# Second norm applied behind the up projection, GpSimd's sums moved to DMA and VectorE, residual and gate loads moved

## The chip, the core and the metric

The kernel runs on one core of a Trainium2 chip. The metric is the time of one execution in microseconds (us). A core has five engines with a queue each, worked off in order: PE (TensorE, matrix products), DVE (VectorE), ACT (ScalarE), POOL (GpSimd) and SP (SyncE, which here only issues DMAs). DMAs issued by SP are those of the profile's queue q1 (hardware_dynamic), those issued by POOL are those of q0 (software_dynamic); in this kernel every DMA of POOL adds its source to its destination.

## What is computed

One layer over 1056 tokens (1024 of a prompt, 8x4 new ones), model width 1024, all in float32:

```
xn = rmsnorm(x, norm1_g);  proj = xn @ w_in          # q, k, v, xr, gr, ga_logit, gr_logit
att = window_attend(q, k, v, ...);  h = rglru(causal_conv(xr, ...))
rnn = (h * gelu(gr)) @ w_o_rnn
mix = (sigmoid(ga_logit) * (att @ w_o_attn) + sigmoid(gr_logit) * rnn) @ w_out
x = x + mix
hmid = relu(rmsnorm(x, norm2_g) @ w_up)              # 1024 -> 4096
x = x + (hmid * hmid) @ w_down                       # 4096 -> 1024
gate = sigmoid(rmsnorm(x, ple_norm_g) @ w_ple_gate)
x = x + gate * (p @ w_ple)
```

rmsnorm(x, g) = x * rsqrt(mean(x*x) + eps) * g, with the mean over the 1024 features of a token.

## The kernel before

Activations lie turned: features on the 128 partitions, the 1056 tokens along a row, so a 1024x1056 matrix is eight tiles [128, 1056]. Each float32 product is made of three matmuls, from a high part (a rounded copy, made by ACT) and a low part (the difference, made by DVE) of both factors: high*high, high*low, low*high.

**First half.** The projections go by chunks of 352 tokens: a chunk is 24 matmuls, and `linear` runs three chunks for one tile of weights. A helper, `Flow`, runs side work between chunks: a generator's `yield n` puts its rest n chunks later. `recur(j)`, j = 0 to 7, is nine chunks: the tiles of xr, gr and ga_logit, with the side work `gates`, whose matmuls (lines 844, 845) take all four PSUM banks `o` and are emptied by ACT (line 847). `turn_x` is side work from j = 2 on: for each of the eight feature tiles it loads x (`xi`), turns it on PE (lines 902, 906) through the same `o` banks, copies it by ACT (903) and stores it in DRAM (`x_dram`), to be read as the residual `X` later.

**Second half.** Ten stages of 28 steps follow: rnn (@ w_o_rnn), out (@ w_out), then up and down four times (here up0, down0, up1, ...; 1024 of the 4096 columns each). A stage is a 1024x1024 product by Strassen's scheme with seven products q = 0 to 6 of half-size blocks, each in four steps p = 0 to 3 of 24 matmuls with 264 tokens (lines 1422 to 1424). Step s of the whole is stage s // 28. `acc`, PSUM, has room for four steps' results.

- Weights: blocks A11, A12, A21, A22 are loaded by SP a stage ahead; their sums (S1 to S4) are made in `down_sums` (stages rnn, out, down: by ACT and POOL's adding DMAs, from eight steps ahead) or in `w_sums` (up0 on POOL, up1 to up3 on DVE). `w_high` (ACT, 1119) and `w_low` (DVE, 1124) split them four and three steps ahead.
- Activations: `b_sums` makes T1 to T4 in place from four blocks b11, b12, b21, b22 (`rnn`, `hid` or `xn` rows), on DVE (1137 to 1142); `b_split` (ACT 1156, DVE 1157) splits them into `ring`, for product q in the first two steps of product q - 1. In up0 the split rows also go to DRAM (`xc_dram`), from where up1 to up3 load them.
- `evacuate` takes a step's result one step later. In rnn it adds into `hid`, and `mix` multiplies by the opened gates (`sigma_of`) and adds `A` (POOL's DMA, 1326). Each gate half row is loaded by SP two steps before its use (1314) into one of four places (two `t`, two halves of `ssq`) and opened by ACT (1317). In out it adds into `X`; a part shared by three blocks is added by POOL's DMA (1247); `squares` has ACT square the finished half row and POOL add it into `ssq` (1180).
- `second_norm(th_)` (for one half of the tokens) sums `ssq` over partitions on PE (1338) and forms the root by ACT and DVE (1339, 245 to 252). `scaled_rows` (DVE, 1350) then makes xn = X * gain * root, from which up0's products start. In the up stages ACT applies Relu and Square to a finished row (1221, 1222).
- `differences` (POOL, 1267) prepares `X` for the down stages. `hooks` says at which step such work is called.

What stands in an engine's queue waits for what stands ahead of it there, so a late operand on DVE or ACT delays the evacuations behind it.

Of the kernel before, what the change touches and what calls it, by code (L numbers as in the profile page):

```python
# [18 lines left out]
P = 128  # L19
# [71 lines left out]
def trunk(ctx: ExitStack, tc: tile.TileContext, I, O):  # L91
# [150 lines left out]

    def rsqrt(r, ms, u):

        ACT.activation(r, ms, AF.Ln)
        ACT.activation(r, r, AF.Exp, scale=-0.5)
        newton(r, ms, u)

    def newton(r, ms, u):
        DVE.tensor_tensor(u, r, ms, op=ALU.mult)  # L250
        DVE.tensor_tensor(u, u, r, op=ALU.mult)  # L251
        DVE.scalar_tensor_tensor(r, u, 3.0, r, op0=ALU.subtract, op1=ALU.mult)

# [637 lines left out]
    def turn_x():  # L891
        for j in range(KT):
# [4 lines left out]
            yield 2  # L897
# [12 lines left out]
    for j in range(KT):  # L910
        if j == 2:
            flow.run(turn_x(), 1)
        recur(j)
# [137 lines left out]
    def kept_place(j2, th_):  # L1051
        return f"d{(2, 3, 0, 1)[j2] if th_ == 0 else (5, 7, 4, 6)[j2]}"
# [6 lines left out]
    def b_view(ph_, k2, kh_, th_):  # L1059

        kind, f = phases[ph_]
        if kind == "rnn":
            return [rnn[4 * kh_ + 2 * k2 + i][:, HALF[th_]] for i in range(2)]
        return [(xn if kind == "up" else hid)[k2 + 2 * kh_][th_]]

    units = {}

    def down_sums(s):

        ph_, at = divmod(s + 8, 28)  # L1070
        if not 0 <= ph_ < NPH or phases[ph_][0] == "up":
            return
# [27 lines left out]
    def w_sums(u):  # L1100
        ph_, q, p2 = u // 28, u % 28 // 4, u % 4 // 2
        if phases[ph_][0] != "up":
            return
        eng = POOL if phases[ph_][1] == 0 else DVE
        v = lambda n: w_view(ph_, n, p2)
        if q == 1:
            eng.tensor_tensor(v("A21"), v("A11"), v("A21"), op=ALU.subtract)
        elif q == 2:
            eng.tensor_tensor(v("S2"), v("A22"), v("S3"), op=ALU.subtract)
        elif q == 5:  # L1110
            eng.tensor_tensor(v("A11"), v("S2"), v("A11"), op=ALU.add)
# [17 lines left out]
    def b_sums(g, k2):  # L1129

        ph_, q = of_product(g)
        kind, f = phases[ph_]
        if kind == "up" and f:
            return
        for b11, b12, b21, b22 in zip(*(b_view(ph_, k2, kh_, th_) for kh_, th_ in ((0, 0), (0, 1), (1, 0), (1, 1)))):
            if q == 2:
                DVE.tensor_tensor(b12, b22, b12, op=ALU.subtract)
                DVE.tensor_tensor(b11, b12, b11, op=ALU.add)
            elif q == 4:
                DVE.tensor_tensor(b21, b21, b11, op=ALU.subtract)  # L1140
            elif q == 5:
                DVE.tensor_tensor(b11, b22, b11, op=ALU.subtract)  # L1142
# [56 lines left out]
    def evacuate(u, ps):  # L1199
# [9 lines left out]
        put = lambda to, of, op: DVE.tensor_tensor(to, of, ps, op=op)  # L1209
        if kind == "up":  # L1210
            if q == 0:
                ACT.copy(q11, ps)
                return
            if q == 1:
                ACT.copy(q12, ps)
            for to, of in (None, [(q11, q11)], [(q12, q12)], [(q22, q12)], [(q21, q22)], [(q22, q22), (q12, q12)], [(q12, q12)])[q]:
                put(to, of, ALU.add)
            h = {1: q11, 4: q21, 5: q22, 6: q12}.get(q)
            if h is not None:
                def squared_relu():  # L1220
                    ACT.activation(h, h, AF.Relu)
                    ACT.activation(h, h, AF.Square)
                flow.later(1, squared_relu)
            return
        if kind == "rnn":

            if q == 0:
                ACT.activation(q11, ps, AF.Identity, scale=-1.0)
                return
            if q == 1:  # L1230
                ACT.activation(q12, ps, AF.Identity, scale=-1.0)
            for to, of, op in (None, [(q11, q11, 0)], [(q12, q12, 1)], [(q22, q12, 0)], [(q21, q22, 1)],
                               [(q22, q22, 1), (q12, q12, 1)], [(q12, q12, 0)])[q]:
                put(to, of, (ALU.subtract, ALU.add)[op])
            if q in (1, 4, 5, 6):
                mix(p + 4 * (q in (4, 5)), q > 4)
            return
        if kind == "out":
# [71 lines left out]

    def loads_gate(j, th_):
        sig = sigmas[len(sigma_of) % 4]
        sigma_of[j, th_] = sig
        SP.dma_start(sig, s_dram[j, :, HALF[th_]])

    def opens_gate(j, th_):
        ACT.activation(sigma_of[j, th_], sigma_of[j, th_], AF.Sigmoid)
# [259 lines left out]
```

## Time and profile before

| | us |
|---|---|
| three runs | 1645.15, 1645.45, 1649.81; median 1645.45 |
| the profiled execution's own time | 1645.47 |
| its span in the profile (first to last instruction) | 1643.7 |
| PE busy in the span | 1560.7 (95%) |
| DVE / ACT / POOL busy | 1066.5 / 859.5 / 365.3 |
| mean granted TensorE clock | 0.984 of full speed |

The profiled execution stands within 0.1 us of the median, so what is read in it is taken off the median directly. PE is busy nearly all the time; what can be gained is where it is not. A granted clock of 1.00 is 2.4 GHz, 0.50 is 1.2 GHz. A stage's borders are found by counting PE's matmuls of lines 1422 to 1424, 672 to a stage.

### The profile page before, as it was taken

How to read it: one execution, taken by the hardware profiler on the slowest of the kernel's cores; microseconds unless marked ns; L12 is line 12 of the kernel's file. 1: busy time of each engine (PE TensorE's matmuls, PEld its weight loads, DVE VectorE, ACT ScalarE, POOL GpSimd, SP SyncE). 2: the span in 40 equal slices, each digit the busy share in tenths (PEclk: the TensorE clock that was granted, in tenths of full speed). 3: DMA queues.
4: the chain of work that ended last, by engine and by line, in shares of the span. 5: the costliest groups of instructions: out<-in, count | busy, mean ns of one | idle time of the engine just before them, and what ended most of it. 6: DMA issues, size and time to landing. Idle time of an engine off the chain costs nothing.

```text
span 1643.7 us, 28183 instructions
## 1 busy us (share of the span) xinstructions
PE 1560.7 (95%) x11488; PEld 1539.8 (94%) x11488; DVE 1066.5 (65%) x1428; ACT 859.5 (52%) x1360; POOL 365.3 (22%) x333
## 2 busy tenths in 40 slices
PE   6989999999899999997967999999999999999997
PEld 5889999999899999997967999999999999999997
DVE  6797565443234441887898888468846884689863
ACT  6555656776677765553444553445344534455441
POOL 4562225222123310220656120001000100012110
PEclk9999999999999999999997999999999999999999
DMA  5422112133232165798922793587358735880332
GB/s 176 78 81 68 53 68 79 52 97 109 89 106 77 42 205 209 151 262 205 199 107 86 287 182 112 203 288 127 113 203 290 125 114 201 292 174 2 99 91 75
DMA packets 177498, 229.30 MB, mean 140 GB/s; under 512 B 21556, under 2 KB 128228, under 8 KB 177352
## 3 DMA queue, kind: packets, MB, share of 16 engines
q1 hardware_dynamic: 148568, 195.83, 35.9%
q0 software_dynamic: 28800, 31.66, 12.0%
q8 instruction: 91, 1.49, 0.4%
q14 instruction: 39, 0.32, 0.1%
HBM read 158.22 MB, written 38.60 MB: 120 GB/s over the span
## 4 chain that ended last, share of the span: by engine, by line
PE 45%; DVE 4%; DMA 2%; issue 1%; ACT 0%; POOL 0%; DVEq 0%; POOLq 0%; ACTq 0%
PE acc L1423 13%; PE acc L1424 13%; PE acc L1422 13%; PE acc L1517 2%; PE acc L1519 2%; PE acc L1518 2%; DMA X<-shared 1%; DVE xn L1350 1%; DVE wul L1124 1%; DVE ring L1157 1%; PE acc L1477 0%; DVE X L1209 0%; DMA out_y_prompt<-yo 0%; POOL ssq L1180 0%; DVE hid L251 0%
## 5 line engine op out<-in xcount | busy, mean ns | idle before, releaser
L1422 PE MATMUL acc<-ring,wuh 128*128 128x264 f32 x2240 | 640.3, 286 | 19.0 <-DVE hid L1209 9.5
L1423 PE MATMUL acc<-ring,wuh 128*128 128x264 f32 x2240 | 642.2, 287 | 5.7 <-DVE ring L1157 5.7
L1424 PE MATMUL acc<-ring,wul 128*128 128x264 f32 x2240 | 642.8, 287 | 0.0
L1422 PEld LDWEIGHTS acc<-ring,wuh 128*128 128x128 f32 x2240 | 426.4, 190 | 20.9 <-DVE hid L1209 9.6
L1423 PEld LDWEIGHTS acc<-ring,wuh 128*128 128x128 f32 x2240 | 424.6, 190 | 7.0 <-DVE ring L1157 6.9
L1424 PEld LDWEIGHTS acc<-ring,wul 128*128 128x128 f32 x2240 | 424.7, 190 | 0.0
L225 PE MATMUL m<-xa,wh 128*128 128x352 f32 x912 | 301.6, 331 | 0.0
L226 PE MATMUL m<-xb,wh 128*128 128x352 f32 x912 | 296.5, 325 | 1.0 <-DVE xb L319 1.0
L227 PE MATMUL m<-xa,wl 128*128 128x352 f32 x912 | 296.9, 326 | 0.0
L1119 ACT CAST wuh<-wblock 128x1024 fp32r<-128x1024 f32 x100 | 104.7, 1048 | 200.7 <-PE acc L1423 161.8
L226 PEld LDWEIGHTS m<-xb,wh 128*128 128x128 f32 x912 | 174.9, 192 | 2.3 <-DVE xb L319 2.0
L225 PEld LDWEIGHTS m<-xa,wh 128*128 128x128 f32 x912 | 174.4, 191 | 1.0 <-ACT xa L318 0.2
L227 PEld LDWEIGHTS m<-xa,wl 128*128 128x128 f32 x912 | 174.0, 191 | 0.0
L1209 DVE TENSOR_TENSOR hid<-hid,acc 128x528 f32<-128x528 f32 x140 | 96.3, 700 | 85.8 <-PE acc L1424 58.8
L1209 DVE TENSOR_TENSOR X<-X,acc 128x528 f32<-128x528 f32 x180 | 121.0, 696 | 36.5 <-PE acc L1424 29.4
L1124 DVE TENSOR_TENSOR wul<-wblock,wuh 128x1024 fp32r<-128x1024 f32 x100 | 127.4, 1274 | 20.6 <-ACT wuh L1119 20.3
L1083 POOL DMA_DIRECT2D wblock<-wblock x12 | 16.1, 1580 | 465.8 <-DMA wblock<-in_w_down 376.4
L1157 DVE TENSOR_TENSOR ring<-hid,ring 128x1056 fp32r<-128x1056 f32 x70 | 89.8, 1282 | 28.7 <-ACT ring L1156 28.7
L1156 ACT CAST ring<-hid 128x1056 fp32r<-128x1056 f32 x70 | 74.1, 1071 | 58.1 <-DVE hid L1142 18.3
L154 DVE TENSOR_TENSOR wl<-wraw,wh 128x1024 fp32r<-128x1024 f32 (+1 forms) x45 | 54.7, 1215 | 49.1 <-ACT wh L153 48.9
L857 DVE SCALAR_TENSOR_TENSOR rt<-a,rt 128x1056 f32<-128x1056 f32 x8 | 10.1, 1258 | 109.1 <-ACT rt L854 109.1
L1180 POOL TENSOR_TENSOR ssq<-ssq,t 128x528 f32<-128x528 f32 x28 | 46.9, 1676 | 133.4 <-ACT t L1179 133.0
(348 smaller groups left out, 2556.1 us busy)
## 6 DMA issues: line engine op xcount, KB each, us to landing
ring<-xc_dram SPq DMA_DIRECT2D x84, 528.0 KB
wblock<-in_w_down SPq DMA_DIRECT2D x40, 512.0 KB
wraw<-in_w_in SPq DMA_DIRECT2D x34, 512.0 KB
wblock<-in_w_up SPq DMA_DIRECT2D x32, 512.0 KB
xc_dram<-ring SPq DMA_DIRECT2D x28, 528.0 KB
wblock<-wblock POOLq DMA_DIRECT2D x24, 512.0 KB, 7.9
s<-wblock POOLq DMA_DIRECT2D x24, 512.0 KB, 5.5
wblock<-in_w_o_rnn SPq DMA_DIRECT2D x10, 512.0 KB
```

The costliest lines, as they stand in the source:

```text
L154: low.tensor_tensor(lo[:, :nk, :], raw[:, :nk, :], f32(hi[:, :nk, :]), op=ALU.subtract)
L225: PE.matmul(ps, wh, xh, start=k == 0, stop=False)
L226: PE.matmul(ps, wh, xl, start=False, stop=False)
L227: PE.matmul(ps, wl, xh, start=False, stop=k == nk - 1)
L1119: ACT.copy(units[u][0], w_view(ph_, PRODUCTS[q][0], p2))
L1124: DVE.tensor_tensor(lo, w_view(ph_, PRODUCTS[q][0], p2), f32(hi), op=ALU.subtract)
L1156: ACT.copy(hi, x)
L1157: DVE.tensor_tensor(lo, x, f32(hi), op=ALU.subtract)
L1209: put = lambda to, of, op: DVE.tensor_tensor(to, of, ps, op=op)
L1422: PE.matmul(ps, wh[:, k, m], r[:, 0, :], start=k == 0, stop=False)
L1423: PE.matmul(ps, wh[:, k, m], r[:, 1, :], start=False, stop=False)
L1424: PE.matmul(ps, wl[:, k, m], r[:, 0, :], start=False, stop=k == 3)
```

## The change

`turn_x` starts one `recur` earlier, loads the next tile right behind the transposes of the last one (four chunks ahead of use in place of two) and takes five chunks per tile in place of four. The gates are loaded in fixed steps, the later ones into rows of `rnn` that are used up, six or more steps before the product that they multiply; the residual's loads go to steps 21 to 29. `b_sums` makes T4 and T1 of rnn, out and up0 by a negation on ACT and adding DMAs of POOL. up0's weight sums go through `down_sums`. The sums of squares of out and `differences` go to DVE. up0's rows are X times the gain alone, made by ACT (`scaled_row`) as each row of out is finished; the root is left in `ssq`, and every up stage multiplies its finished row by it on DVE (with the relu in the same instruction), and ACT squares that. The sign of the root (-2 times it is kept) is taken out by the square's scale of 0.5. In PE's queue the transposes of `turn_x` stood right behind a group of `gates` matmuls at three places before and stand so at one now.

```
+    def rsqrt(r, ms, u, to=None):
...
+        DVE.scalar_tensor_tensor(r if to is None else to, u, 3.0, r, op0=ALU.subtract, op1=ALU.mult)
...
     def turn_x():
...
+        xi, xj = load(0)
+        yield 3
+        for j in range(KT):
             xo = big.tile([P, T], F32, tag="e6", name="xo")
             for h in range(2):
                 ps = bank()
                 for t in range(4):
                     PE.transpose(ps[:, t * P:(t + 1) * P], xi[:, 4 * h + t, :], ident)
                 ACT.copy(xo[:, h * 512:(h + 1) * 512], ps)
-                yield 1
+                if h == 0:
+                    yield 1
             ps = bank()
             PE.transpose(ps[:, :NS], xj, ident[:NS, :NS])
             ACT.copy(xo[:, NP:], ps[:, :NS])
+            if j + 1 < KT:
+                xi, xj = load(j + 1)
+            yield 1
             SP.dma_start(x_dram[j], xo)
+            yield 3
     for j in range(KT):
-        if j == 2:
+        if j == 1:
             flow.run(turn_x(), 1)
...
+    def later_up(ph_):
+        kind, f = phases[ph_]
+        return kind == "up" and f > 0
...
         ph_, at = divmod(s + 8, 28)
-        if not 0 <= ph_ < NPH or phases[ph_][0] == "up":
+        if not 0 <= ph_ < NPH or later_up(ph_):
...
+        if not later_up(ph_):
...
         v = lambda n: w_view(ph_, n, p2)
         if q == 1:
-            eng.tensor_tensor(v("A21"), v("A11"), v("A21"), op=ALU.subtract)
+            DVE.tensor_tensor(v("A21"), v("A11"), v("A21"), op=ALU.subtract)
...
+        by_dma = kind != "down"
         for b11, b12, b21, b22 in zip(*(b_view(ph_, k2, kh_, th_) for kh_, th_ in ((0, 0), (0, 1), (1, 0), (1, 1)))):
...
+            elif q == 3 and by_dma:
+                ACT.activation(b11, b11, AF.Identity, scale=-1.0)
+                POOL.dma_start(b21, b11, accum_op=ALU.add)
+            elif q == 4 and by_dma:
+                POOL.dma_start(b11, b22, accum_op=ALU.add)
             elif q == 4:
                 DVE.tensor_tensor(b21, b21, b11, op=ALU.subtract)
-            elif q == 5:
+            elif q == 5 and not by_dma:
                 DVE.tensor_tensor(b11, b22, b11, op=ALU.subtract)
...
+    def squares(j, th_, eng):
...
-            POOL.tensor_tensor(ssq2[:, o], ssq2[:, o], s, op=ALU.add)
+            eng.tensor_tensor(ssq2[:, o], ssq2[:, o], s, op=ALU.add)
...
+            sign = 1.0 if later_up(ph_) else -1.0
+            add, neg = ALU.add, ALU.add if later_up(ph_) else ALU.subtract
+            if q < 2:
+                ACT.activation((q11, q12)[q], ps, AF.Identity, scale=sign)
+            for to, of, op in ([], [(q11, q11, neg)], [(q12, q12, add)], [(q22, q12, neg)], [(q21, q22, add)],
+                               [(q22, q22, add), (q12, q12, add)], [(q12, q12, neg)])[q]:
+                put(to, of, op)
+            if q not in (1, 4, 5, 6):
                 return
-            if q == 1:
...
-            if h is not None:
-                def squared_relu():
-                    ACT.activation(h, h, AF.Relu)
-                    ACT.activation(h, h, AF.Square)
...
+            h, r = (q12, q11, q21, q22)[(6, 1, 4, 5).index(q)], ssq[:, HALF[th_]].rearrange("p (c n) -> p c n", c=2)
+            def squared_relu():
+                DVE.scalar_tensor_tensor(h, h, 0.0, r, op0=ALU.max, op1=ALU.mult)
+                ACT.activation(h, h, AF.Square, scale=0.5)
+            flow.later(1, squared_relu)
...
             if q in (1, 4, 5, 6):
-                flow.later(1, lambda: squares(p + 4 * (q in (4, 5)), int(q > 4)))
+                j, th_ = p + 4 * (q in (4, 5)), int(q > 4)
+                flow.later(1, lambda: (squares(j, th_, DVE), scaled_row(j, th_)))
...
         for x in (x12, x21):
-            POOL.tensor_tensor(x, x, x22, op=ALU.subtract)
+            DVE.tensor_tensor(x, x, x22, op=ALU.subtract)
...
-        rsqrt(hid[2 + th_][0][:, 0], ssq[:, HALF[th_]], hid[2 + th_][0][:, 1])
-    def scaled_rows(j2, th_):
-        xn[j2][th_] = big.tile([P, 2, TH], F32, tag=kept_place(j2, th_), name="xn")
-        for i in range(2):
-            j = 2 * j2 + i
-            DVE.scalar_tensor_tensor(xn[j2][th_][:, i], X[j][:, HALF[th_]], g2h[:, j:j + 1], hid[2 + th_][0][:, 0],
-                                     op0=ALU.mult, op1=ALU.mult)
+        rsqrt(hid[2 + th_][0][:, 0], ssq[:, HALF[th_]], hid[2 + th_][0][:, 1], ssq[:, HALF[th_]])
...
+    def scaled_row(j, th_):
+        if xn[j // 2][th_] is None:
+            xn[j // 2][th_] = big.tile([P, 2, TH], F32, tag=kept_place(j // 2, th_), name="xn")
+        ACT.activation(xn[j // 2][th_][:, j % 2], X[j][:, HALF[th_]], AF.Identity, scale=col("g2", j))
...
-    sigma_of = {}
-    for q, m, th_ in ((1, 0, 0), (4, 1, 0), (5, 1, 1), (6, 0, 1)):
-        for p in range(4):
...
-    hook(28 + 21, second_norm, 0)
-    hook(28 + 22, scaled_rows, 2, 0)
...
+    for j in range(4):
+        hook(2 + j, sigmoid, j, 0)
+        hook(10 + j, load_sigma, j + 4, 0, rnn[j][:, HALF[1]])
+        hook(12 + j, lambda j=j: load_sigma(j + 4, 1, sigmas[j]))
+        hook(14 + j, sigmoid, j + 4, 0)
+        hook(15 + j, load_sigma, j, 1, rnn[j + 4][:, HALF[0]])
+        hook(18 + j, sigmoid, j + 4, 1)
+        hook(21 + j, load_residual, j)
+        hook(22 + j, sigmoid, j, 1)
+        hook(26 + j, load_residual, j + 4)
+        hook(84 + j, differences, j)
+    hook(28 + 23, second_norm, 0)
     hook(28 + 30, summed.clear)
-    hook(56 + 1, second_norm, 1)
...
-        hook(56 + s, scaled_rows, j2, 1)
+    hook(56 + 2, second_norm, 1)
...
     hid = [[hidden_rows(j2, h, F32, "hid") for h in range(2)] for j2 in range(4)]
+    for j in range(4):
+        load_sigma(j, 0, sigmas[j])
...
         down_sums(s)
-        if ph_ == FIRST_UP and q > 3 and p % 2 == 0 and q < 6:
-            differences(2 * (q - 4) + p // 2)
```

The places that the diff alone does not show are in the engines' queues. A row is the line, the operation, and output<-inputs with partitions x elements; rows of before carry its line numbers, rows of after its own. First POOL from the end of stage out (the last sums of squares in `ssq`, the last `shared` parts added to `X`) through up0. Before, up0's weight sums (1107 to 1113) and `differences` (1267) stood there as POOL's own arithmetic:

```order
L1180 TENSOR_TENSOR ssq<-ssq,t_6558 128x528
L1107 TENSOR_TENSOR wblock<-wblock 128x4x256
L1180 TENSOR_TENSOR ssq<-ssq,t_6557 128x528
L1109 TENSOR_TENSOR s_6427<-wblock 128x1024
L1109 TENSOR_TENSOR s_6428<-wblock 128x1024
L1111 TENSOR_TENSOR wblock<-s_6427,wblock 128x4x256
L1111 TENSOR_TENSOR wblock<-s_6428,wblock 128x4x256
L1267 TENSOR_TENSOR X<-X 128x528 x2
```

Now POOL's arithmetic is gone from these stages, and adding DMAs stand in its queue: those of the weight sums (1096 to 1111), with those of the row sums T4 (1154) and T1 (1156) between them:

```order
L1259 DMA X<-shared 128x528 x8
L1096 DMA wblock<-wblock 128x4x256 x2
L1102 DMA s_6427<-wblock 128x4x256
L1102 DMA s_6428<-wblock 128x4x256
L1108 DMA wblock<-wblock 128x4x256 x2
L1154 DMA xn<-xn 128x1056 x2
L1111 DMA s_6427<-wblock 128x4x256
L1111 DMA s_6428<-wblock 128x4x256
L1156 DMA xn<-xn 128x1056 x2
```

What moved: 30 arithmetic instructions of POOL left its queue (14 sums of squares, 8 `differences`, 8 weight sums), and 24 adding DMAs came in: eight of 128x528 in rnn, four of 128x1056 each in out and up0, and eight of 512 KB for up0's weight sums; the issues stand ahead of later ones in the order shown.

Second DVE at the seam, where the second half's root (`mean_square`, 1339 before, 1353 after; the root's last steps 250 to 252) is formed in up0's first steps. Before, eight scaled rows (1350) stood between the root and the row sums (1137, 1138):

```order
L1124 TENSOR_TENSOR wul<-wblock,wuh 128x1024
L1339 TENSOR_SCALAR ssq<-acc 128x528
L250 TENSOR_TENSOR hid<-hid,ssq 128x528
L251 TENSOR_TENSOR hid<-hid 128x528
L252 SCALAR_TENSOR_TENSOR hid<-hid 128x528
L1157 TENSOR_TENSOR ring_6426<-xn,ring_6426 128x2x528
L1350 SCALAR_TENSOR_TENSOR xn<-X,g2h,hid 128x528 x4
L1124 TENSOR_TENSOR wul<-wblock,wuh 128x1024
L1350 SCALAR_TENSOR_TENSOR xn<-X,g2h,hid 128x528 x4
L1137 TENSOR_TENSOR xn<-xn 128x1056
L1138 TENSOR_TENSOR xn<-xn 128x1056
```

Now the root goes into `ssq`, no scaled row follows, and the splits and row sums that stood behind them follow at once, with the last sum of squares (1198) ahead:

```order
L1198 TENSOR_TENSOR ssq<-ssq,t_6555 128x528
L1136 TENSOR_TENSOR wul<-wblock,wuh 128x1024
L1175 TENSOR_TENSOR ring_6426<-xn,ring_6426 128x2x528
L1353 TENSOR_SCALAR ssq<-acc 128x528
L250 TENSOR_TENSOR hid<-hid,ssq 128x528
L251 TENSOR_TENSOR hid<-hid 128x528
L252 SCALAR_TENSOR_TENSOR ssq<-hid 128x528
L1136 TENSOR_TENSOR wul<-wblock,wuh 128x1024
L1150 TENSOR_TENSOR xn<-xn 128x1056
L1151 TENSOR_TENSOR xn<-xn 128x1056
L1175 TENSOR_TENSOR ring_6423<-xn,ring_6423 128x2x528
L1150 TENSOR_TENSOR xn<-xn 128x1056
```

What moved: 16 scaled rows left DVE (eight of them here), and its 14 sums of squares came in, between the evacuations of out's last 16 steps.

## Rows read from the trace of the kernel before

**Rows 1.** Busy time by stretch: stretch, length, engines' busy us, granted clock, DMA share, GB/s.
```profile
662.76:745.28 82.52, 82.17 (x672) 81.98 (x673) 66.64 (x93) 41.89 (x62) 20.88 (x20) 1.00 0.87 211
745.28:771.35 26.07, 17.73 (x121) 17.14 (x121) 18.01 (x22) 7.68 (x9) 2.58 (x2) 0.87 1.00 250
771.35:844.76 73.41, 69.61 (x558) 68.47 (x557) 62.79 (x64) 34.10 (x42) 32.45 (x26) 1.00 0.63 146
844.76:902.85 58.09, 38.77 (x244) 37.20 (x245) 48.84 (x38) 24.23 (x34) 38.45 (x18) 0.79 0.24 97
902.85:955.64 52.79, 52.79 (x434) 52.79 (x433) 43.94 (x47) 34.63 (x43) 9.02 (x5) 1.00 0.80 275
1037.77:1119.91 82.14, 82.14 (x675) 82.14 (x673) 45.13 (x50) 43.15 (x58) 5.18 (x4) 1.00 0.75 246
```

**Rows 2.** Waits of PE, 690 to 1000 us: us in total, times, longest us.
```profile
PE acc L1422 <- DVE hid L1209: 9.5, 3, 8.8
PE acc L1422 <- DVE X L1209: 7.9, 3, 6.5
PE acc L1338 <- POOL ssq L1180: 7.8, 2, 6.3
```

**Rows 3.** Waits of PE to 560 us, the same columns.
```profile
PE o L902 <- DMA xi<-in_x_prompt: 7.0, 3, 4.6
PE o L902 <- ACT it L847: 3.4, 2, 1.7
...
PE o L906 <- ACT it L847: 1.7, 1, 1.7
```

**Rows 4.** Timeline of PE, 429.7 to 435.3: start, us, instruction, idle before and releaser.
```profile
429.78 0.32 PE L226 MATMUL m<-xb,wh 128*128 128x352 f32 x1
429.94 0.32 PE L227 MATMUL m<-xa,wl 128*128 128x352 f32 x1
434.84 0.87 PE L902 MATMUL o<-ident,xi 128*128 128x128 f32 x3 [4.58 <-DMA xi<-in_x_prompt]
```

**Rows 5.** Busy time in the stretches at the lower clock, columns of rows 1.
```profile
433.10:439.90 6.80, 5.06 (x19) 5.09 (x20) 0.88 (x1) 2.95 (x3) 0.00 (x0) 0.50 0.59 190
887.10:900.70 13.60, 7.31 (x31) 7.00 (x32) 11.08 (x9) 7.81 (x13) 8.95 (x4) 0.50 0.39 159
```

**Rows 6.** Timeline of ACT, 753 to 762 us.
```profile
760.42 0.64 ACT L1317 ACTIVATE ssq<-ssq 128x528 f32<-128x528 f32 x1 [6.10 <-DMA ssq<-s_dram]
```

**Rows 7.** Groups of 740 to 910 us: busy us, mean ns | idle before, releasers.
```profile
L1180 POOL TENSOR_TENSOR ssq<-ssq,t 128x528 f32<-128x528 f32 x14 | 25.0, 1784 | 48.0 <-ACT t L1179 47.9
L1209 DVE TENSOR_TENSOR X<-X,acc 128x528 f32<-128x528 f32 x24 | 16.3, 695 | 7.2 <-DMA X<-shared 3.9 <-ACT shared L1242 3.1
```

**Rows 8.** Single lines, whole span: ns min/median/max, first and last start us.
```profile
L1124 DVE TENSOR_TENSOR wul<-wblock,wuh x100: 1209/1219/2354, 658.7 to 1508.8; 128x1024 fp32r<-128x1024 f32 x100
...
L1157 DVE TENSOR_TENSOR ring<-xn,ring x14: 1246/1258/3181, 840.5 to 940.4; 128x1056 fp32r<-128x1056 f32 x14
...
L1350 DVE SCALAR_TENSOR_TENSOR xn<-X,g2h,hid x16: 754/760/2907, 832.0 to 881.3; 128x528 f32<-128x528 f32 x16
...
L1221 ACT ACTIVATE hid<-hid x64: 626/643/650, 892.2 to 1450.4; 128x528 f32<-128x528 f32 x64
```

**Rows 9.** Line 1095, POOL's adding DMAs of 512 KB, from issue to landing.
```profile
DMA to landing us min/median/max: 5.1/5.7/8.9
```

**Rows 10.** DMA queues, 792 to 798 us: packets, MB, share of the DMA engines.
```profile
q0 software_dynamic: 1087, 1.13, 121.1%
```

**Rows 11.** DMA queues, 802 to 816 us.
```profile
q0 software_dynamic: 1016, 1.92, 74.2%
q1 hardware_dynamic: 869, 1.67, 35.3%
```

**Rows 12.** DMA queues, 740 to 760 us.
```profile
q1 hardware_dynamic: 2437, 4.45, 63.6%
q0 software_dynamic: 1355, 1.60, 47.3%
```

More of the change, by code (lines that the diff above doesn't have):

```diff
@@ L241, in linear, with newton @@
             flow.step()
-    def rsqrt(r, ms, u):
+    def rsqrt(r, ms, u, to=None):
         ACT.activation(r, ms, AF.Ln)
         ACT.activation(r, r, AF.Exp, scale=-0.5)
-        newton(r, ms, u)
-    def newton(r, ms, u):
+        newton(r, ms, u, to)
+    def newton(r, ms, u, to=None):
         DVE.tensor_tensor(u, r, ms, op=ALU.mult)
         DVE.tensor_tensor(u, u, r, op=ALU.mult)
-        DVE.scalar_tensor_tensor(r, u, 3.0, r, op0=ALU.subtract, op1=ALU.mult)
+        DVE.scalar_tensor_tensor(r if to is None else to, u, 3.0, r, op0=ALU.subtract, op1=ALU.mult)
     ACT.preload_act_table_set("natural_log_exp_and_others")
@@ L891, in turn_x, with load @@
     def turn_x():
-        for j in range(KT):
+        def load(j):
             xi = big.tile([P, T], F32, tag="e7", name="xi")[:, :D].rearrange("p (t d) -> p t d", t=8)
@@ L896, in turn_x @@
             SP.dma_start(xj, xs[:, j * P:(j + 1) * P])
-            yield 2
+            return xi, xj
+        xi, xj = load(0)
+        yield 3
+        for j in range(KT):
             xo = big.tile([P, T], F32, tag="e6", name="xo")
@@ L1101, in w_sums @@
         ph_, q, p2 = u // 28, u % 28 // 4, u % 4 // 2
-        if phases[ph_][0] != "up":
+        if not later_up(ph_):
             return
-        eng = POOL if phases[ph_][1] == 0 else DVE
         v = lambda n: w_view(ph_, n, p2)
         if q == 1:
-            eng.tensor_tensor(v("A21"), v("A11"), v("A21"), op=ALU.subtract)
+            DVE.tensor_tensor(v("A21"), v("A11"), v("A21"), op=ALU.subtract)
         elif q == 2:
-            eng.tensor_tensor(v("S2"), v("A22"), v("S3"), op=ALU.subtract)
+            DVE.tensor_tensor(v("S2"), v("A22"), v("S3"), op=ALU.subtract)
         elif q == 5:
-            eng.tensor_tensor(v("A11"), v("S2"), v("A11"), op=ALU.add)
+            DVE.tensor_tensor(v("A11"), v("S2"), v("A11"), op=ALU.add)
         elif q == 6:
-            eng.tensor_tensor(v("S2"), v("A12"), v("S2"), op=ALU.subtract)
+            DVE.tensor_tensor(v("S2"), v("A12"), v("S2"), op=ALU.subtract)
     def w_high(u):
@@ L1173, in trunk @@
     summed = set()
-    def squares(j, th_):
+    def squares(j, th_, eng):
         x, o = X[j][:, HALF[th_]], HALF[th_]
@@ L1185, in third_high @@
     def third_high(j, th_):
-        squares(j, th_)
+        squares(j, th_, POOL)
         x = X[j][:, HALF[th_]]
@@ L1209, in evacuate @@
         put = lambda to, of, op: DVE.tensor_tensor(to, of, ps, op=op)
-        if kind == "up":
-            if q == 0:
-                ACT.copy(q11, ps)
-                return
-            if q == 1:
[L1215 to L1218, printed above, removed]
-            if h is not None:
-                def squared_relu():
-                    ACT.activation(h, h, AF.Relu)
-                    ACT.activation(h, h, AF.Square)
[L1223 to L1228, printed above, removed]
-                return
[L1230 to L1236, printed above, removed]
+        if kind in ("rnn", "up"):
+            sign = 1.0 if later_up(ph_) else -1.0
[6 more added lines that the diff above has]
+            if q not in (1, 4, 5, 6):
+                return
+            th_ = int(q > 4)
+            if kind == "rnn":
+                mix(p + 4 * (q in (4, 5)), th_)
+                return
+            h, r = (q12, q11, q21, q22)[(6, 1, 4, 5).index(q)], ssq[:, HALF[th_]].rearrange("p (c n) -> p c n", c=2)
[3 more added lines that the diff above has]
+            flow.later(1, squared_relu)
             return
@@ L1308, in prepare_b, with load_sigma, sigmoid @@
                 b_sums(gg, SUMS_AT[p])
[L1311 to L1316, printed above, removed]
+    sigma_of = {}
+    def load_sigma(j, th_, place):
+        sigma_of[j, th_] = place
+        SP.dma_start(place, s_dram[j, :, HALF[th_]])
+    def sigmoid(j, th_):
         ACT.activation(sigma_of[j, th_], sigma_of[j, th_], AF.Sigmoid)
@@ L1397, in trunk @@
     POOL.memset(ones, 1.0)
-    g2h = late.tile([P, KT], F32, name="g2h")
-    DVE.tensor_scalar(g2h, col("g2", 0, KT), -0.5, None, op0=ALU.mult)
     ssq2 = ssq = late.tile([P, T], F32, name="ssq")
```

8 lines of the change are left out of this document (removed).

## The prediction

> **What bounds the kernel now.** I read the page's busy times, then the busy time by stage, the waits of PE, and around each long wait the timelines of the engines it names; durations and DMA rates last. PE is the bound: it is busy 95% of the span, so only the time in which it stands or runs at the lower clock can be won. [Rows 1] say where. A stage that nothing holds up, up1, lasts 82.14 us: 28 steps of 2.93 us. Against that pace rnn loses 0.4 us (82.52 less 82.14), out's first five steps 11.4 (26.07 less 5 x 2.934 = 14.67), its other 23 steps 5.9 (73.41 less 67.5) and up0's first ten 28.8 (58.09 less 29.3). The rest of up0 and up1 lose nothing. Sum: 46.5 us.
>
> The waits [rows 2] name three releasers. *Gates.* ACT stood 6.10 us for a gate half row, `ssq` from `s_dram` [rows 6]; DVE's evacuations are queued behind the multiplication by that gate, so PE found no free `acc` (the 6.5 us in rows 2). In that stretch the DMA engines are full, share 1.00 [rows 1], since the residual's rows go out ahead of the gates. *POOL's arithmetic.* A sum of squares takes POOL 1784 ns where DVE takes 695 for an addition of the same shape [rows 7], and PE waits 6.3 us for the last of them before the second root. While POOL computes, DVE's own instructions reach 2354 ns in place of 1219 (1124), 3181 in place of 1258 (1157) and 2907 in place of 760 (1350) [rows 8], so the two seem to hold each other up. *The root.* The scaled rows wait for it, and up0's products for them: the 8.8 us of rows 2. After it PE ran 13.6 us at granted 0.50, the 1.2 GHz level [rows 5].
>
> The first half is untouched but for `turn_x`. There PE waits 7.0 us for `xi`, 4.6 at most, and 3.4 + 1.7 = 5.1 for ACT to empty the `o` banks, at three places [rows 3]. Behind the 4.58 us wait [rows 4] a stretch ran at 0.50 with 5.06 us of PE work [rows 5], 2.5 of it owed to the clock.
>
> **The change, part by part.**
>
> *turn_x.* A chunk is 24 matmuls starting 0.16 us apart [rows 4], 3.8 us. A load two chunks ahead had 7.6 us; the longest wait shows that it needed 12.2; four chunks give 15.3. So -7.0, and with the wait the half clock, -2.5. Of three places behind `gates` one stays: -3.4 of 5.1. That tile's last transpose now asks for a fifth bank at once: +0.6, about one ACT copy (0.64 in rows 6 for a like width). Together -12.3; if the DMA queues were as late as before, only -3.4.
>
> *Second half, removed.* The three releasers all go: gates are loaded six or more steps ahead (17.6 us, against waits of 6), POOL computes nothing in these stages, and up0's rows need no root. I take off the whole 46.5 and ask what is late next.
>
> *Adding DMAs of POOL.* T4, T1 and the weight sums now share one queue. In rnn, out and up0 it is to move, from step 7 on, A11's sums (2 x 0.52 MB), T4 (1.08), S2's (1.05) and T1 (1.08): 4.26 MB. T4 can be issued about 22 us in (its rows are negated in the product before), T1 has to be there at step 20, 58.7 us in. Less 3.5 us for ACT and DVE to split it and 2.3 for landing (5.1 us for the fastest 512 KB alone [rows 9], of which 2.8 is bytes), 31 us are left: 137 GB/s needed. What the queue reached: 188 GB/s alone (1.13 MB in 6 us, [rows 10]), 137 beside loads of weight blocks (1.92 in 14, [rows 11]), 80 beside full-row loads (1.60 in 20, [rows 12]). So the price lies between nothing and 4.26 / 0.080 - 31 = 22 us a stage.
>  - up0 stores 28 split rows to `xc_dram` meanwhile, more than blocks, less than rows 12: I take the middle of 137 and 80, 108, hence 39.4 us, +8.
>  - rnn has two `A` additions more in the queue (4.8 MB), beside the early gates: 137, hence 35 us, +4.
>  - out has few loads, but `X<-shared` joins (12 x 0.27 MB): 7.5 MB from 22 us until the first root asks for the rows they complete, step 23 of out (67.5 us) less 2.3 for landing and 0.7 for an evacuation: 42.5 us. Between 188 and 137 I take 162: 46.3, +4.
>
> *DVE at the seam.* From out's q = 4 to up0's q = 1 (20 steps, 58.7 us) DVE gets: eight steps of 2.64 us (two additions of 0.70, half of a 1.22 and of a 1.26), four of q = 5 with a third addition, 3.34; two roots, 2.8 each; four steps of 1.24 with 5.0 of row sums; four of q = 1 at 2.70. Sum: 21.1 + 13.4 + 5.6 + 10.0 + 10.8 = 60.9, that is 2.2 us over the time, where the scaled rows would have added 12. It stands in order behind the roots, which wait for PE's sum (1338) at a step's distance: I add one step's DVE work, 2.6, for each. +7; nothing if PE's four `acc` places cover it, 11 (what out's start cost through the same chain) if not. What is queued behind the root's wait: w_low and the splits of the next product, then PE.
>
> *Rest.* `differences` on DVE, 8 x 0.7 us over four steps at the start of down0; the stretch before has DVE busy 43.94 of 52.79 us [rows 1], so some of it stays visible: +1. In the up stages 64 multiplications of about 0.76 us (1350's form) come to DVE, 12 us a stage beside 45.13 of 82.14 busy [rows 1]: hidden; 64 Relu of 0.643 (1221) leave ACT. The 16 scaled rows on ACT (0.65 each) lie beside 24.23 of 58.09 busy. None is charged; if the up stages' results came late by one instruction each, DVE would still be ahead of the evacuation a step later.
>
> *Sum.* 1645.5 (the profiled execution, 0.1 above the median) - 12.3 - 46.5 + 8 + 4 + 4 + 7 + 1 = 1610.7, so **1611 us**.
>
> One place where a page is weighed: rows 9 have 5.1 us at least and 5.7 in the middle for 512 KB. The Trainium skill (DMA: Bandwidth & Descriptors, "Anatomy of one DMA — SWDGE (gpsimd) path") fits about 2.0 us plus bytes over 436 GB/s to one such DMA, an estimate of 3.2 us here. By it the sums would be in time everywhere, and the result would be the first rival's. The trace does not agree, and the measurement decides: these DMAs read and add at their destination.
>
> **The rivals.**
>
> *All sums in time* (1595). If the queue runs at 137 GB/s or more in all three stages, only the seam's 7 and the 1 stay: 1645.5 - 58.8 + 8 = 1594.7. For it: 188 alone, and out's DMA share of 0.63 and up0's 0.24 before [rows 1]. Against it: up0's new 6.35 MB come on top.
>
> *POOL's queue becomes the bound* (1679, slower). In order and at 80 GB/s, T1 arrives 22 us late in up0, 60 - 31 = 29 in rnn and 22 in out; PE stands, and the clock falls behind it as it did at 887 us, some 11 us more (two such places at half of 13.6, less what hides). 58.8 off, 73 + 11 + 8 on: +33. It decides against the change once the sums are late by more than 58.8 - 8 = 51 us in all, which is at 93 GB/s or less (13.32 MB in 93 + 51 us). For it: 80 measured where full rows load beside it. Against it: only rnn's start looks like that stretch, and by T4 the early gates have landed. The Trainium skill (DMA: Bandwidth & Descriptors, "Issuing engines are not separate DMA queues") says that transfers of all issuing engines run on the same 16 engines and interleave; the trace agrees: the queue fell from 188 to 137 GB/s as soon as the other one moved 1.67 MB beside it [rows 10, 11].
>
> *The gates or the seam are not cleared* (1622). The four early gates, or the later ones, still share full DMA engines with weights and residual, and out's start keeps its 11.4; or DVE, 61 us of work for 58.7 us, holds up0's first ten steps for as much: 1611 + 11 = 1622, with both 1633. For it: share 0.87 in rnn, 1.00 behind it [rows 1]. Against it: six steps of lead.
>
> *No change.* It would need gains and losses to cancel, between 1640.5 and 1650.4.
>
> **How the numbers follow.** Forecast (1601 to 1620) 0.45; all in time (1588 to 1601) 0.27; gates or seam (1620 to 1636) 0.16; no change 0.04; slower 0.08. A measurement of this kernel can tell about 0.3%, 4.9 us, so faster is below 1640.5: 0.45 + 0.27 + 0.16 = 0.88; same 0.04; slower 0.08. The range 1588 to 1634 leaves out the slower case, no change and the ends of the others, 0.15 or so. The likeliest case's own range is 1601 to 1620.
>
> **What would show it.** turn_x: no wait of its transposes for a DMA, and no half clock near 433. Gates: ACT does not stand for `s_dram` rows, and out's first five steps take 14.7. Sums: PE or the casts into `ring` wait for adding DMAs of `gl`, `hid` and `xn` at q = 4 and 5 of the three stages, most in up0, and the queue's rate there is near 108 to 162 GB/s. Seam: DVE busy nearly without a gap from out's q = 4 on, and its instructions at their short times, none of 2.3 or 3.2 us. It would be wrong if up0's first ten steps lasted over 45 us (29.3 + 8 + 7), if waits for POOL's DMAs added up to more than 50 us, or if PE, now running on, met a wait in the up or down stages that before had none.

## The result and the profile after

The changed kernel takes 1638.05 us, median of four runs (1636.45 to 1638.54), against 1646.76 for the kernel before (1645.15 to 1649.81): ratio 0.9943, interval 0.9925 to 0.9961. It is faster by 9 us, where 34 were forecast (1611; range 1588 to 1634).

The profiled execution took 1636.45 us, span 1634.7. Busy time by stage, columns as in [rows 1]: rnn, out's first five steps, the rest of out, up0, down0, up1.

```profile
649.25:741.14 91.89, 85.40 (x673) 84.62 (x673) 64.84 (x88) 46.61 (x69) 27.82 (x28) 0.96 0.92 215
741.14:755.81 14.67, 14.67 (x123) 14.67 (x122) 14.43 (x19) 4.06 (x4) 2.60 (x2) 1.00 1.14 278
755.81:842.02 86.21, 74.85 (x558) 72.31 (x557) 56.69 (x67) 49.24 (x63) 21.71 (x22) 0.94 0.87 190
842.02:938.75 96.73, 88.64 (x678) 86.17 (x677) 67.39 (x80) 51.16 (x64) 13.90 (x12) 0.96 0.95 280
938.75:1028.48 89.73, 84.98 (x672) 84.00 (x673) 78.40 (x92) 29.81 (x31) 7.69 (x6) 0.98 0.53 128
1028.48:1110.60 82.12, 82.12 (x674) 82.12 (x673) 54.83 (x65) 33.47 (x42) 5.15 (x4) 1.00 0.74 243
```

rnn begins at 649.25 us, 13.5 earlier than before: that is `turn_x` (in the other kernels with the same `turn_x` it begins at 649.67 to 653.82, so 13.5 is the upper end of 8.9 to 13.5). out's first five steps, 26.07 before, take 14.67, the undisturbed pace. But from rnn's start to the end of down3's matmuls it is 872.2 us, where it was 868.0. The 46.5 us are gone from their places, and 50.5 have come in others. Step by step, what a step took over 2.935 us (from its first matmul to that of the next, so a wait just before step 20 counts to step 19):

| place (steps of the whole) | lost, us | forecast |
|---|---|---|
| rnn, q = 4 and 5 (16 to 20) | 9.7 | 4 |
| out, q = 1 and 2 (35, 36) | 5.4 | 0 |
| out, q = 2 to 5 (39 to 49) | 5.1 | 4 |
| the seam (51 to 59, 63 to 68) | 14.9 | 7 |
| up0, q = 4 to 6 (75 to 83) | 7.8 | 8 |
| down0, q = 0 to 2 (84 to 93) | 7.6 | 1 |

PE's waits from 640 to 1000 us (total, times, longest) name VectorE now, not GpSimd and not the root as in [rows 2]:

```profile
PE acc L1432 <- DVE hid L1227: 12.0, 6, 5.7
PE acc L1432 <- DVE X L1227: 9.4, 4, 3.8
PE acc L1352 <- DVE X L1227: 3.3, 1, 3.3
PE acc L1433 <- DVE ring L1175: 2.5, 3, 1.2
```

The name is only the last link. In rnn the waits of all engines from 690 to 722 us read, from the end of the chain to its start:

```profile
PE acc L1432 <- DVE hid L1227: 5.7, 1, 5.7
DVE ring L1175 <- ACT ring L1174: 16.2, 6, 8.9
ACT ring L1174 <- DMA gl<-gl: 19.8, 7, 8.5
```

and the timeline of ACT there:

```profile
700.75 0.64 ACT L1331 ACTIVATE gl<-gl 128x528 f32<-128x528 f32 x1
709.86 0.63 ACT L1174 CAST ring<-gl 128x528 fp32r<-128x528 f32 x1 [8.47 <-DMA gl<-gl]
711.90 0.63 ACT L1174 CAST ring<-gl 128x528 fp32r<-128x528 f32 x1 [1.41 <-DMA gl<-gl]
```

The cast of T1 stands in ACT's queue, VectorE's half of the split waits for it, and the evacuations are queued behind that. PE did all 24 matmuls of step 19 and stood before the first of step 20, which needs T1 and a free `acc` place. T1's first half was split at 713.27, and the place came free at 715.02. The timelines of PE and of VectorE there:

```profile
709.17 0.28 PE L1434 MATMUL acc<-ring,wul 128*128 128x264 f32 x1
715.17 0.56 PE L1432 MATMUL acc<-ring,wuh 128*128 128x264 f32 x1 [5.71 <-DVE hid L1227]
```

```profile
712.56 0.71 DVE L1175 TENSOR_TENSOR ring<-gl,ring 128x528 fp32r<-128x528 f32 x1 [1.33 <-ACT ring L1174]
713.19 1.22 DVE L1136 TENSOR_TENSOR wul<-wblock,wuh 128x1024 fp32r<-128x1024 f32 x1
714.32 0.70 DVE L1227 TENSOR_TENSOR hid<-hid,acc 128x528 f32<-128x528 f32 x1
```

How long T1's additions (line 1156) took from issue to landing, in all three stages, and the two pieces of rnn in the chain of work that ended last (start, us):

```profile
DMA to landing us min/median/max: 14.1/20.0/21.9
```

```profile
676.80 12.94 DMA gl<-gl
...
690.02 21.86 DMA gl<-gl
```

The clock falls behind such waits: from 698 to 722 us 0.86 was granted, which is the loss of step 20.

```profile
698.00:722.00 24.00, 17.94 (x123) 17.38 (x124) 13.19 (x18) 11.69 (x17) 2.60 (x4) 0.86 0.95 228
```

Of the two pieces of the chain the first is T4's. It reads the row that T1 then overwrites, so T1 is issued only after it has landed: two landings in series, where [rows 9] had 5.7 us for one. POOL's timeline has the issues in that order, T4 (1154), two weight sums (1111), T1 (1156):

```profile
676.25 3.11 POOL L1154 DMA_DIRECT2D gl<-gl  x2
677.34 2.91 POOL L1340 DMA_DIRECT2D hid<-A  x1
677.88 4.13 POOL L1154 DMA_DIRECT2D gl<-gl  x2
680.68 2.66 POOL L1111 DMA_DIRECT2D s<-wblock  x1
684.60 1.28 POOL L1111 DMA_DIRECT2D s<-wblock  x1 [1.27 <-DMA wblock<-wblock]
688.40 0.88 POOL L1156 DMA_DIRECT2D gl<-gl  x1 [2.52 <-DMA gl<-gl]
690.02 0.86 POOL L1156 DMA_DIRECT2D gl<-gl  x1 [0.73 <-DMA gl<-gl]
694.18 0.86 POOL L1156 DMA_DIRECT2D gl<-gl  x1 [3.31 <-DMA gl<-gl]
697.70 0.86 POOL L1156 DMA_DIRECT2D gl<-gl  x1 [2.66 <-DMA gl<-gl]
```

POOL's queue from 674 to 712 us, when the last of T1 had landed, and in up0 from 872 to 910 us:

```profile
q0 software_dynamic: 3577, 4.86, 75.7%
```

```profile
q0 software_dynamic: 2688, 4.26, 64.1%
```

That is 128 GB/s in rnn and 112 in up0, near the 137 and 108 that I took: the queue was not slow, T1 was late in it. In up0 T1's addition takes 20 us in the chain of work that ended last:

```profile
889.62 20.09 DMA xn<-xn
909.77 1.08 ACT ring L1174
```

### The profile page after: what moved, and what is told of

Read it like the earlier page. It is cut to its first block, busy times and chain, and to the rows that moved or that the text cites. A ratio compares the mean times of both kernels' runs of the same rounds, so it can differ in the third digit from the quotient of the medians.

```text
span 1634.7 us, 28211 instructions
## 1 busy us (share of the span) xinstructions
PE 1561.1 (95%) x11488; PEld 1537.9 (94%) x11488; DVE 1072.1 (66%) x1481; ACT 838.7 (51%) x1324; POOL 329.6 (20%) x327
## 4 chain that ended last, share of the span: by engine, by line
PE 72%; DVE 10%; DMA 8%; ACT 5%; issue 3%; POOL 1%; SPq 1%; ACTq 0%; POOLq 0%; DVEq 0%
PE acc L1433 12%; PE acc L1432 12%; PE acc L1434 12%; PE m L225 9%; PE m L227 9%; PE m L226 9%; DMA gl<-gl 2%; PE acc L1527 2%; PE acc L1529 2%; PE acc L1528 2%; DMA xn<-xn 2%; DMA X<-shared 2%; DVE wul L1136 1%; DVE ring L1175 1%; DMA wblock<-in_w_out 1%
## 5 line engine op out<-in xcount | busy, mean ns | idle before, releaser
L1136 DVE TENSOR_TENSOR wul<-wblock,wuh 128x1024 fp32r<-128x1024 f32 x100 | 122.0, 1220 | 18.8 <-ACT wuh L1131 18.8
L1247 ACT ACTIVATE hid<-hid 128x528 f32<-128x528 f32 x64 | 41.3, 645 | 92.0 <-DVE hid L1246 92.0
```

The lines of the kernel that those rows point to most:

```text
L1136: DVE.tensor_tensor(lo, w_view(ph_, PRODUCTS[q][0], p2), f32(hi), op=ALU.subtract)
```

## The experiments

My first theory: the late T4 and T1 make most of the 50.5 us, and `turn_x` is the whole gain. The rival: VectorE is the bound, and the sums' place doesn't matter. Medians in us; ratio to the kernel before, run beside each; "second half" is from rnn's start to the end of down3's matmuls in the profile, one execution (868.0 before, 872.2 after, 821 undisturbed). The first half differs by up to 4.6 us between these profiles, so a price in the second half is read there, and a difference of 1 or 2 us between medians tells nothing.

| run | median | ratio, interval | second half |
|---|---|---|---|
| e1_turn | 1633.8 | 0.9924 (0.9909 to 0.9939) | 869.1 |
| e2_dve_T | 1612.1 | 0.9791 (0.9776 to 0.9806) | 844.4 |
| e3_pool_w | 1638.2 | 0.9946 (0.9929 to 0.9962) | 872.5 |
| e4_resid_late | 1632.9 | 0.9914 (0.9896 to 0.9931) | 866.1 |
| e5_diff_pool | 1615.7 | 0.9816 (0.9802 to 0.9831) | 850.9 |
| e6_T1_first | 1628.0 | 0.9891 (0.9876 to 0.9905) | 863.4 |
| e7_all | 1606.4 | 0.9761 (0.9745 to 0.9778) | 839.8 |
| e8_sq_pool | 1615.7 | 0.9815 (0.9800 to 0.9829) | 849.0 |
| e9_gates | 1624.5 | 0.9857 (0.9840 to 0.9873) | 859.9 |
| e10_norm | 1620.3 | 0.9834 (0.9819 to 0.9848) | 855.9 |
| e11_diff_early | 1605.3 | 0.9743 (0.9729 to 0.9758) | 839.5 |
| e12_root_late | 1606.3 | 0.9753 (0.9738 to 0.9768) | 840.3 |

**e1_turn.** The kernel before with the change's `turn_x`, begun at `j == 1`.

> The kernel before with the new turn_x alone. Theory: the first half's gain is the whole gain of the change; rnn starts 13.5 us earlier in the profile of the changed kernel (649.25 for 662.76), and the second half is not faster (872.2 us from rnn's start to the end of down3's matmuls, 868.0 before). So 1632 to 1635, some 4 us under the changed kernel. Rival: rnn's early start only moves the transfers of the second half closer together, and part of the 13.5 is lost again behind it: 1638 to 1642.

1633.8: the theory. This part alone stands some 4 us under the whole change (the two intervals overlap; in the profiles the second half is 869.1 against 872.2). So `turn_x` alone is worth the change's whole net gain.

**e2_dve_T.**
```
-        by_dma = kind != "down"
+        by_dma = False
```


> The changed kernel with T4 and T1 of rnn, out and up0 made by VectorE, as before; POOL's queue loses 24 - 8 = 16 adding DMAs (6.5 MB). Theory 1: the late adding DMAs are the cost (9.7 us at q = 4 and 5 of rnn, 6.6 at q = 4 and 5 of up0, the 7.2 at down0's start as their aftermath, part of out's 5): 1615 to 1622. Rival: VectorE is the bound, the sums' 0.7 and 1.25 us come back to it (15.6 us in all) and the wait only changes its name: 1634 to 1640.

1612.1, 26 us under the changed kernel, and 3 below the theory's range: theory 1, and more than it had. rnn's 9.7 are gone, up0's 7.8 shrink to 0.4, steps 51 and 52 go from 8.2 to 2.2 (`X<-shared`, in the same queue, lands in 7.6 us in place of 14.0, medians). Down0's loss stays, 7.5: it is not an aftermath of T1, as theory 1 had it.

**e3_pool_w.** `down_sums` leaves out up0 again, `w_sums` does its sums with `eng = POOL if phases[ph_][1] == 0 else DVE`, signs as before.

> The changed kernel with up0's weight sums made by GpSimd's arithmetic as before, in place of eight adding DMAs (and two reloads of weights). Theory 1: POOL's DMA queue in up0 is too slow by these 4.2 MB; T1 of up0 comes in time, up0's 6.6 us at q = 4 and 5 and the 7.2 at down0 go: 1624 to 1630. Rival: the queue is held up by the stores of split rows, not by its own load, and GpSimd's arithmetic lengthens VectorE's instructions again to 2 or 3 us: 1638 to 1646.

1638.2, unchanged: the rival's number. Its first reason, the stores, falls, and its second comes at a size that it did not have. T1 of up0 was in time and the waits at steps 75 to 77 went, but 7.2 us came at steps 71 and 72. The timelines of VectorE and of GpSimd there:

```profile
893.45 10.90 DVE L1137 TENSOR_TENSOR wul<-wblock,wuh 128x1024 fp32r<-128x1024 f32 x1
```

```profile
893.56 5.06 POOL L1124 TENSOR_TENSOR wblock<-s,wblock 128x1024 f32<-128x1024 f32 x2
898.26 5.00 POOL L1126 TENSOR_TENSOR s<-wblock,s 128x1024 f32<-128x1024 f32 x2
```

One split of 1.22 us lasted 10.90, to 904.35, some 1.1 us past the end of GpSimd's four instructions (903.26).

**e4_resid_late.**
```
-        hook(26 + j, load_residual, j + 4)
+        hook(34 + j, load_residual, j + 4)
```

(With a guard for rows of `X` that are not yet loaded.)

> The changed kernel with the second half of the residual's loads (rows 4 to 7, 2.2 MB) eight steps later, at steps 34 to 37 in place of 26 to 29. Theory: out's weight block loaded at step 33 and the sums made of it wait behind the residual in the queue of loads; the 5.4 us at out's q = 1 and 2 go: 1632 to 1634. Rival: the adding DMAs themselves are slow there, 5.4 stay, and the later residual makes out's q = 3 wait: 1637 to 1642.

1632.9: the theory. Steps 35 and 36 lose nothing, and q = 3 didn't wait more. The changed residual loads had taken the place of the gates in front of weight blocks.

**e5_diff_pool.** e2_dve_T with `POOL.tensor_tensor` in `differences`, called at up0's q = 4 and 5 as before.

> The kernel of e2_dve_T (1612.1) with differences made by GpSimd in up0's q = 4 and 5, as in the kernel before. Theory: the 7.5 us that e2_dve_T still loses at down0's start (steps 87 to 92) are VectorE's: it works there without a gap, with 8 x 0.7 us of differences added; they go: 1603 to 1606. Rival: GpSimd's arithmetic lengthens VectorE's instructions in up0, and it gives back what down0 wins: 1610 to 1616.

1615.7: the rival's number, with the theory's mechanism right too. Down0's loss fell from 7.5 to 1.7, but steps 66 and 67 lost 13.3 in place of 1.4, by one multiplication of VectorE and eight subtractions of GpSimd:

```profile
860.58 11.20 DVE L1246 SCALAR_TENSOR_TENSOR hid<-hid,ssq 128x528 f32<-128x528 f32 x1
```

```profile
861.08 11.84 POOL L1280 TENSOR_TENSOR X<-X 128x528 f32<-128x528 f32 x8
```

**e6_T1_first.**
```
-        elif at == 17:
+        elif at == 21:
```


> The changed kernel with POOL's last adding DMAs for the weights (at = 17) four steps later, behind those of T1 instead of ahead of them; nothing else. Theory: T1 is late by what stands ahead of it in POOL's own queue, 1.05 MB at about 98 GB/s, 10 us; the 9.7 us of rnn and up0's 6.6 go, out gains little: 1620 to 1625. Rival 1: the transfers of the other queue beside it set the pace of every addition, and the order in the queue matters little: 1633 to 1640. Rival 2: the weight sums are late instead, at product 6: 1630 to 1638.

1628.0, ten less, though 3 above the theory's range. T1's landings (line 1156) halved by the order in the queue alone:

```profile
DMA to landing us min/median/max: 8.6/10.3/13.9
```

rnn's loss fell from 9.7 to 0.4, up0's from 7.8 to 0.5: there the theory holds against rival 1. out lost more (steps 35 and 36: 11.7 for 5.4), as in rival 2 but not at product 6: ACT waits 18.9 us there for a weight sum whose additions stood behind late loads:

```profile
ACT wuh L1131 <- DMA s<-wblock: 18.9, 1, 18.9
POOL s L1102 <- DMA s<-in_w_out: 16.2, 1, 16.2
```

That PE reached out early does not explain it: in e2_dve_T, where rnn holds it up as little (out starts at 735.83 us, here at 735.23), these steps lose 4.3. So the rest probably comes from what stands in POOL's queue here, the moved weight sums or T4 and T1; the two were not tried apart.

**e7_all.** e2_dve_T with e4_resid_late's edit and `hook(70 + 3 * j, differences, j)`.

> The kernel of e2_dve_T with two things more: residual rows 4 to 7 loaded eight steps later (as e4_resid_late, which gained 5), and differences, still on VectorE, at up0's steps 14 to 23, where e2_dve_T has no waits, in place of down0's first four. Theory: out's 4.3 and down0's 7.5 go, nothing comes for them: 1599 to 1603. Rival: VectorE has no room in up0 either, and the differences' 5.6 us show there: 1605 to 1609.

1606.4: the theory misses by 3, the rival's range has it. out's 4.3 go, down0 falls from 7.5 to 2.4, but 4.1 come at steps 79 to 83, most of what the rival said.

**e8_sq_pool.** e2_dve_T with `squares(j, th_, POOL)` in out.

> The kernel of e2_dve_T with out's sums of squares on GpSimd, as before; VectorE loses 14 x 0.7 us in the 16 steps of the seam. Theory: GpSimd's 1.78 us each, and the two engines lengthening each other's instructions, cost more than the 9.8 us of VectorE are worth: PE waits for the last sum before each root again, 7.8 us in the kernel before: 1615 to 1622. Rival: VectorE is the bound at the seam (60.9 us of work for 58.7), and what e2_dve_T loses at steps 51 to 68 (14 us) shrinks: 1604 to 1610.

1615.7, the theory's low end: steps 51 to 59 lose 14.5 in place of 5.9, steps 63 to 68 1.9 in place of 4.9. GpSimd's help at the seam costs more than it gives, 4.6 us in the second half (the intervals of the ratios overlap a little). The 60.9 us of work for 58.7 that the rival took over from the prediction are not what VectorE does there; see below.

**e9_gates.** e1_turn with `load_sigma`, `sigmoid`, `load_residual` and their hooks of the change.

> The kernel before with the new turn_x (e1_turn, 1633.8) and the change's schedule of gate and residual loads; the second norm, all sums and GpSimd's arithmetic as before. Theory: the late gates were the cause of out's slow first five steps, 11.7 us in e1_turn, and early ones take them away; of it about 4.3 come back at out's q = 1 and 2, as in e2_dve_T, where the residual now stands ahead of a weight block: 1624 to 1628. Rival: the residual and weights simply wait in the gates' place, and nothing is won: 1631 to 1636.

1624.5: the theory. Steps 28 to 32 lose nothing; 4.9 come at 35 and 36.

**e10_norm.** e8_sq_pool with the edits of e3_pool_w and e5_diff_pool: e9_gates and the second norm moved.

> e9_gates with the second norm moved behind the up projection as in the change, GpSimd's sums of squares, weight sums and differences still as before, T4 and T1 on VectorE. Theory: the scaled rows and PE's 8.8 us behind the root are the larger part of up0's 28.8 us, and go; GpSimd's slow arithmetic still costs the 16 to 17 us that e5_diff_pool and e8_sq_pool show at steps 51 to 68: 1610 to 1618. Rival: GpSimd's arithmetic is the bound of up0's start whatever the norm does, and little of the 28.8 goes: 1620 to 1626.

1620.3: the rival, at its edge. Of up0's 28 us in e9_gates 24 remain without one scaled row; they stand beside GpSimd's arithmetic (in VectorE's timeline one split, at 836.78 us, lasts 3.40, one sum, at 848.93, 3.32). In e2_dve_T, where GpSimd has no arithmetic there, up0 loses 8.4. So the root's wait, which I had named as one of three causes, was mostly cover for this one.

**e11_diff_early.** e7_all with `hook(68 + 2 * j, differences, j)`.

> e7_all (1606.4) with differences at up0's steps 12 to 18 (q = 3 and 4) in place of 14 to 23. Theory: the 4 us that e7_all loses at steps 79 to 83 are VectorE's backlog in q = 5 and 6, where the multiplications by the root stand; further ahead VectorE has room: 1602 to 1604. Rival: VectorE has no room at q = 3 and 4 either: 1605 to 1608.

1605.3, not to be told from e7_all: the rival.

**e12_root_late.**
```
-    hook(28 + 23, second_norm, 0)
+    hook(28 + 30, second_norm, 0)
...
-    hook(56 + 2, second_norm, 1)
+    hook(56 + 10, second_norm, 1)
```


> e11_diff_early with the two roots later: the first from step 51 to 58, the second from 58 to 66, still ahead of the rows that are multiplied by them (steps 61 and 77). Theory: VectorE at the seam is the bound, and the roots' 2 x 2.8 us with their waits in its queue are what PE loses at steps 51, 52, 58, 59 (4.9 us) and part of 63 to 68 (4.9): 1595 to 1600. Rival: VectorE's work is the same, so the loss only moves some steps on: 1602 to 1604.

1606.3: the rival, 2 above its range. Steps 51 to 59 lose 1.4 in place of 5.9, steps 63 to 67 10.2 in place of 4.6: the loss moves, wherever the roots stand. That VectorE's work is the bound does not follow: from step 44 to 68 it is busy 67.0 of 85.2 us here and 67.0 of 84.4 in e11_diff_early, and in most of the rest it waits for ACT, 16.3 and 17.0 us.

## Why the prediction was wrong

- **turn_x** was right: -12.3 forecast, 13.5 in the profile, some 13 in e1_turn. No transpose waits for a DMA any more.
- **The 46.5 us** were rightly given to gates, GpSimd and root, and are gone. What each is worth can be priced only net of what comes in its place: the gates 9 us (e9_gates against e1_turn, by the medians and in the second half), the second norm's move alone 4, not the larger part. GpSimd's arithmetic, taken from e10_norm to e2_dve_T, gives 8 more by the medians and 11.5 in the second half, with what VectorE takes over already paid.
- **The step that failed** is the window of the adding DMAs: "T4 can be issued about 22 us in", and with T1 there at step 20 "31 us are left: 137 GB/s needed". The window's end held: PE stood before the first matmul of step 20 in rnn, of step 48 in out (2.06 us from one matmul to the next) and of step 76 in up0 (2.65), where it needs T1. The rates nearly held (128 and 112 GB/s for 137 and 108). What failed is that the sums were taken as megabytes that flow through the whole window. The runs showed in its place: T4's first addition was issued 27 us into rnn, 34 into out and 35 into up0; T1's can't start before T4's has landed; and T1 stood behind 1.05 MB of weight sums. So T1 took 20.0 us to land, where its 1.08 MB at 137 GB/s and the 2.3 us give 10, and where e6_T1_first, with the weight sums behind it, has 10.3. The 16 us forecast for late sums became 26 to 28 (e2_dve_T), and the order in the queue alone gives back ten, net of what out loses by it (e6_T1_first). What T1's wait for T4 costs by itself was not tried. That up0's loss came out as forecast, 7.8 for 8, is partly luck, since T4 came 13 us later there than assumed.
- **The seam** was mis-sized: 7 forecast, 10.8 in e2_dve_T, where no sum is late. The reason given, 60.9 us of VectorE's work in 58.7, is wrong. In these 20 steps VectorE was busy 53.5 us of 66.2 (the third busy time of the row below; its instructions overlap a little, one of 0.70 us being followed after 0.62), and the sign that I had named, VectorE busy nearly without a gap, did not come. For most of the other 12.7 us it stood in its queue for ACT, half of that for ACT's part of the splits. The stretch of e2_dve_T, and VectorE's waits in it:

```profile
787.96:854.19 66.23, 61.97 (x490) 60.26 (x488) 53.48 (x64) 45.12 (x58) 10.28 (x10) 1.00 0.81 210
```

```profile
DVE ring L1175 <- ACT ring L1174: 6.0, 4, 3.1
DVE hid L250 <- ACT hid L246: 3.4, 2, 1.9
DVE ssq L1198 <- ACT t L1197: 3.0, 4, 0.8
```

  So VectorE's queue is what PE waits for, but its waits for ACT belong to it as much as its work. Which of them would have to go was not tried.
- **differences** were mis-sized: +1 forecast; of the 7.5 that down0 loses in e2_dve_T, 5.8 go with them (e5_diff_pool), since VectorE comes to down0 with up0's last multiplications still ahead of it. From 947 to 974 us it worked 26.13 of 27.00 us:

```profile
947.00:974.00 27.00, 22.27 (x164) 21.49 (x163) 26.13 (x32) 9.74 (x11) 5.12 (x4) 0.94 0.64 121
```

  The multiplications that I called hidden in the up stages are so in up1 (54.83 of 82.12 busy, nothing lost), and not at up0's end: steps 83 to 93 lose nothing in e9_gates, without them, and 2.8 in e10_norm, with them; both have `differences` on GpSimd.
- **Not in the sum at all**: out's weight block behind the moved residual, 5.4 (e4_resid_late). I had priced what the loads give the gates, not what they take from the next in their queue.

The terms leave 50.5 us in place of 24: 26.5 of the 27 by which the time was missed. The slower rival was nearer than my 0.08 made it: T1 was late in all three stages, and the clock fell behind the waits. But its mechanism, the queue at 93 GB/s or less, did not come; what made T1 late is its place in the queue. Its sum was also too low for out: at 80 GB/s the forecast's own 7.5 MB in 42.5 us are 51 us late, not 22.

The best version here is e11_diff_early with e7_all beside it: 1605.3, 0.9743 of the kernel before. It keeps `turn_x`, the early gates, the moved norm and VectorE's squares, and takes T4 and T1 back to VectorE. What is still lost there, 18 us, is nearly all from step 51 on, where PE waits for VectorE's queue.

## What to carry to other kernels

A sum moved to DMA is not free because its engine is: count from when its operands are ready, what it waits for and what stands ahead of it in its queue; a rate over the whole window hides all three. A sum of an engine's work is no bound either, as long as it leaves out what the engine waits for in its queue. Try each part of a change alone: here one part was worth the whole net gain, and another took back 26 us of the rest.

## What the runs showed of the hardware

Two times a row of GpSimd instructions of two inputs that followed each other without a gap held up a single VectorE instruction for nearly as long as the row lasted: 0.71 us became 11.20 beside eight, 1.22 became 10.90 beside four (e5_diff_pool, e3_pool_w). Before, I had read only 2 to 3 us of this in [rows 8]. It is not so for every row: in e10_norm VectorE's instructions beside four of the same `differences` took 1.73 and 1.81 us, and what decides between the two is not shown. The timelines of GpSimd and VectorE there:

```profile
872.11 6.62 POOL L1281 TENSOR_TENSOR X<-X 128x528 f32<-128x528 f32 x4
```

```profile
875.84 1.73 DVE L1176 TENSOR_TENSOR ring<-xn,ring 128x1056 fp32r<-128x1056 f32 x1 [0.26 <-ACT ring L1175]
877.49 1.81 DVE L1247 SCALAR_TENSOR_TENSOR hid<-hid,ssq 128x528 f32<-128x528 f32 x1
```

The Trainium skill (SBUF — State Buffer, "SBUF: two separate sides") says that the two share a port pair, held by one of them for a whole instruction while the other blocks; the traces agree on the blocking, but in those two places it lasted over a whole row of instructions, not one.
